# A two-block transformer kernel on one core: the first mixer's convolution, its tap engines and its place between the mLSTM's heads

## The chip, the cores and the metric

The kernel runs on one core of one Trainium2 chip. The time is device microseconds of that core from launch to end, the median of three runs. TensorE is called PE here, VectorE DVE, ScalarE ACT, GpSimd POOL and SyncE SP.

## What is computed

Two stacked blocks of two layers each on 512 tokens of width 1024, with a context of 256 tokens in the first block. The change lies in the first layer's mixer of the first block, which works on all 768 tokens. The part of the reference that matters:

```
a, g, q, k, v, o, gates = split(h @ w_in)
u = dwconv(a * sigmoid(g), conv_w (31 taps, 512 channels), conv_b)
u = silu(layer_norm(u, ln_g, ln_b))
h_seq = mLSTM(q, k, v, gates), forward and backward, 4 heads
        h = num / max(|den|, exp(-m_row))        per head and direction
hm = rms(h_seq) * head_gain * sigmoid(o)
y = concat(u, hm) @ w_out
```

Everything is float32 in and out. A product with weights is three matmuls on PE: each operand is split into a high and a low part of the type fp32r, and high by high, high by low and low by high are added in PSUM. ACT makes the high part of a weight chunk (`whi`, line 287), DVE the low part (`wlo`, line 288).

## The kernel before, in words

Channels (or tokens, inside the mLSTM) lie on the 128 partitions. `mixer0` (line 684) builds the first mixer. One *product* (`fmk_g`, line 385, which calls `fm_g`, line 369) takes one 512 KB chunk of weights, 1024 columns wide, and makes 128 output channels for all 768 tokens: 24 matmuls of 512 columns and 24 of 256.

The 512 channels of the convolution are four blocks of 128. `conv_g` (line 786) makes one block: two products (gate `g` and value `a`; those of block 0 are made earlier, by `first`), a tanh on ACT (line 797), the gated value `up` on DVE (line 801), and then 31 taps over 783 columns (both token segments with padding). With `NPOOL = 10` the taps stand on three engines: DVE does 21 of a block (line 813 the first, line 821 twenty others, each `acc = up[shifted] * weight + acc`), ACT scales ten shifted copies (lines 815 and 818), POOL adds nine of them up in `acc2` (line 819) and adds that to `acc` at the end (line 824). `convt`, the tile between ACT and POOL, has two buffers. `conv_norm` (line 828) is the layer norm over the four blocks: POOL sums the blocks (lines 833 and 835), PE and DVE make the mean, DVE centres (line 855), ACT squares (line 862), POOL sums the squares (line 864), DVE scales (line 870) and adds `ln_b` (line 874), and then comes the SiLU.

The *output gates* are four more products, `th[0]` to `th[3]`, one for each head, with a tanh on ACT (line 717).

The convolution and the gates are one generator, `work` (line 707). `more(n)` (line 782) advances it n steps, and `mixer0` calls it between the four q and k products (`MORE`, line 962), and `mlstm` in each pass. The written order is blocks 0 to 3, gates 0 and 1, the norm, gates 2 and 3. That order is a priority only: a scheduler places each instruction on its engine by its own estimate of the times, and engines then run in the order that it fixed, with semaphores between them. SP loads the weight chunks; the adaptive-norm products of later layers (line 525, `ps_ad`, one 512 KB chunk for two matmuls of 512 columns that run at float32 rate) are a second side work.

`mlstm` (line 964) goes over 4 heads with 6 *passes* each (one for each 128 tokens): PE makes scores (line 997), ACT the decay factors with exp (lines 1014, 1016), DVE multiplies them (line 1021), PE multiplies by v with a column of ones (line 1034), and DVE normalises the result of the pass: copy of the denominators, absolute value, maximum, reciprocal, scaling of the first direction, second direction added (lines 1037 to 1042). Passes 0 and 1 of a head look at 2 blocks of keys, the other four at 6. `v1` is copied out of PSUM by DVE (line 741). At a head's end its result is transposed on PE (line 1056) and multiplied by its output gate (line 1057). The output projection (`ab_o`, from line 747) takes the four convolution blocks as its first four chunks and the heads as the last four.

PSUM has three banks tagged `ml` for scores and results; a pass of six key blocks takes two.

## Time and profile before

| what | us |
|---|---|
| median of three runs | 3781.64 (3776.6 to 3785.46) |
| profiled execution, its own time | 3775.19 |
| its span, first to last instruction | 3773.4 |
| PE busy in the span | 3643.6 |
| first scores of the mLSTM (line 997) | at 246.84 |
| last passes of the mLSTM end, last head transposed | about 424 |

All times in rows are microseconds from the span's start. "Busy" is the time in which an engine has an instruction in work; matmuls overlap, so a matmul's own duration is longer than the step to the next. PEclk is the share of 2.4 GHz that PE was granted; it is 1.0 or 0.5, and values between are means over a stretch. A wait's releaser is inferred from semaphore events.

### The profile page before, as it was taken

To read this page: it belongs to the slowest core of one execution; us is meant where nothing else is said; L and a number is where in the kernel's file an instruction comes from. 1 tells how busy PE (TensorE), PEld (TensorE's weight loads), DVE (VectorE), ACT (ScalarE), POOL (GpSimd) and SP (SyncE) were. 2 spreads that over 40 slices of the span, in tenths; PEclk is the share of its full clock that TensorE was granted. 3 is DMA by queue.
4 is the path that set the end of the run, shared out by engine and by line. 5 is a ranking of instruction groups with operands and counts; after the bars stand their busy time and mean duration, and the time that the engine had idled before them with its cause. 6 is when DMAs were issued, how large, how long until landed. Compare 5 with 4: busy or idle time off the path is not lost. (4 is left out here: it accounts for less than half of the span.)

```text
span 3773.4 us, 50278 instructions
## 1 busy us (share of the span) xinstructions
PE 3643.6 (97%) x19848; PEld 2979.0 (79%) x19848; DVE 2191.9 (58%) x3583; ACT 1430.5 (38%) x2507; POOL 543.4 (14%) x528
## 2 busy tenths in 40 slices
PE   7889999999999999999999999999999999999998
PEld 5667877888877667888877888888887888888887
DVE  6986454444456666655576565555566656545545
ACT  4335332222235555433354333432234433333222
POOL 3540100000025221000221110300022111020001
PEclk9989999999999999999999999999999999999999
DMA  5223323332211010333333322233324333222232
GB/s 194 72 78 115 104 90 117 118 123 63 67 49 44 22 34 23 103 103 96 97 111 101 96 86 77 78 100 101 95 73 130 96 98 93 73 90 90 95 96 78
DMA packets 107388, 336.88 MB, mean 89 GB/s; under 512 B 14864, under 2 KB 19600, under 8 KB 106896
## 3 DMA queue, kind: packets, MB, share of 16 engines
q1 hardware_dynamic: 94864, 316.88, 26.2%
q10 hardware_dynamic: 12288, 16.79, 1.8%
q8 instruction: 156, 2.56, 0.3%
q14 instruction: 80, 0.66, 0.1%
HBM read 310.54 MB, written 2.10 MB: 83 GB/s over the span
## 5 line engine op out<-in xcount | busy, mean ns | idle before, releaser
L287 ACT CAST whi<-raw 128x1024 fp32r<-128x1024 f32 (+2 forms) x488 | 501.7, 1030 | 1148.6 <-PE ps_mm L367 698.6
L288 DVE TENSOR_TENSOR wlo<-raw,whi 128x1024 fp32r<-128x1024 f32 (+2 forms) x488 | 621.6, 1276 | 370.4 <-ACT whi L287 367.6
L367 PE MATMUL ps_mm<-h,whi 128*128 128x512 f32 (+2 forms) x2593 | 642.3, 354 | 20.1 <-ACT cth L797 10.6
L367 PE MATMUL ps_mm<-xg,whi 128*128 128x512 f32 (+1 forms) x1929 | 571.9, 378 | 9.1 <-DVE xg L302 7.0
L367 PEld LDWEIGHTS ps_mm<-h,whi 128*128 128x128 f32 (+1 forms) x2593 | 428.1, 189 | 108.5 <-issue 17.8
L367 PE MATMUL ps_mm<-hid,whi 128*128 128x512 f32 (+1 forms) x1805 | 469.5, 357 | 0.0
L367 PEld LDWEIGHTS ps_mm<-xg,whi 128*128 128x128 f32 x1929 | 357.1, 189 | 80.0 <-DVE xg L302 11.4
L367 PE MATMUL ps_mm<-h,wlo 128*128 128x512 f32 (+2 forms) x1298 | 393.9, 353 | 0.5 <-DVE wlo L288 0.5
L366 PE MATMUL ps_mm<-xg,whi 128*128 128x512 f32 (+1 forms) x1207 | 373.9, 388 | 2.7 <-DVE xg L302 2.7
L367 PE MATMUL ps_mm<-xg,wlo 128*128 128x512 f32 (+1 forms) x966 | 362.0, 377 | 0.5 <-DVE wlo L288 0.5
L367 PEld LDWEIGHTS ps_mm<-hid,whi 128*128 128x128 f32 x1805 | 310.3, 188 | 59.3 <-issue 6.7
L367 PE MATMUL ps_mm<-hid,wlo 128*128 128x512 f32 (+1 forms) x903 | 298.9, 356 | 0.0
L366 PEld LDWEIGHTS ps_mm<-xg,whi 128*128 128x128 f32 x1207 | 219.9, 189 | 49.3 <-issue 5.3
L367 PEld LDWEIGHTS ps_mm<-h,wlo 128*128 128x128 f32 (+1 forms) x1298 | 217.4, 189 | 36.2 <-DVE wlo L288 1.0
L366 PE MATMUL ps_mm<-xg,wlo 128*128 128x512 f32 (+1 forms) x602 | 228.4, 382 | 0.0
L367 PEld LDWEIGHTS ps_mm<-xg,wlo 128*128 128x128 f32 x966 | 182.9, 190 | 33.8 <-DVE wlo L288 1.0
L367 PEld LDWEIGHTS ps_mm<-hid,wlo 128*128 128x128 f32 x903 | 160.4, 189 | 24.9
L1532 POOL TENSOR_TENSOR rsw<-rsw,rope 128x512 f32<-128x512 f32 x64 | 107.7, 1683 | 428.5 <-DMA rsw<-rsw 286.5
L1156 DVE SCALAR_TENSOR_TENSOR xl<-ps_mm,mod,xl 128x512 f32<-128x512 f32 (+1 forms) x102 | 73.0, 717 | 110.7 <-PE ps_mm L367 110.2
L366 PE MATMUL ps_mm<-whi,xg 128*128 128x512 f32 x384 | 132.0, 414 | 0.0
L366 PEld LDWEIGHTS ps_mm<-xg,wlo 128*128 128x128 f32 x602 | 113.8, 189 | 22.2 <-issue 0.7
L821 DVE SCALAR_TENSOR_TENSOR acc<-up,cw,acc 128x783 f32<-128x783 f32 x80 | 124.4, 1555 | 2.2
(572 smaller groups left out, 5833.4 us busy)
## 6 DMA issues: line engine op xcount, KB each, us to landing
raw<-in_fup SPq DMA_DIRECT2D x88, 512.0 KB, 3.5
raw<-in_sup SPq DMA_DIRECT2D x88, 512.0 KB, 3.5
raw<-in_ada SPq DMA_DIRECT2D x80, 512.0 KB, 3.6
raw<-in_l_qk SPq DMA_DIRECT2D x48, 512.0 KB, 3.5
raw<-in_fdn SPq DMA_DIRECT2D x32, 512.0 KB, 3.5
raw<-in_d_v SPq DMA_DIRECT2D x32, 512.0 KB, 3.6
raw<-in_d_gt SPq DMA_DIRECT2D x32, 512.0 KB, 3.5
raw<-in_sdn SPq DMA_DIRECT2D x32, 512.0 KB, 3.5
```

The source lines that it names most:

```text
L287: self.nc.scalar.copy(h[:, :n], r[:, :n])
L288: (lo or self.nc.vector).tensor_tensor(l[:, :n], r[:, :n], h[:, :n].bitcast(F32), ALU.subtract)
L366: return self.nc.tensor.matmul(out, w, x, **k)
L367: return self.nc.tensor.matmul(out, w, x, **k)
L821: nc.vector.scalar_tensor_tensor(acc, u, s, acc, ALU.mult, ALU.add)
L1156: self.pin(nc.vector.scalar_tensor_tensor(xs, o[:, : b - a], self.m(layer, 5, d, int(a < TC)), xs, ALU.mult, ALU.add))
L1532: nc.gpsimd.tensor_tensor(sw, sw, self.SR, ALU.mult)
```

## The change

All 31 taps of a block go to DVE; ACT's scaled copies and POOL's sums of them are gone, with the tiles `conv2` and `convt` for taps. The sums of `conv_norm` (blocks, squares) move from POOL to DVE. The written order of the side work becomes blocks 0 to 2, gates 0 and 1, block 3, the norm, gates 2 and 3, with other step counts (`MORE`). Four pieces move from DVE to ACT: the copies of v, the absolute value of the denominators (one instruction for two), the scaling of the first direction, and the addition of `ln_b`.

```
@@ -705,18 +705,25 @@
             accs, th, mixc = [], [], []
 
             def work():
-                for j in range(4):
-                    accs.append((yield from self.conv_g(mp, j, hs, cw, None if j else made)))
-                yield
-                for j in range(4):
-                    if j == self.NORM:
-                        yield from self.conv_norm(mp, accs, mixc)
+                def gate(j):
                     t = pair()
                     o = yield from self.fmk_g(I["ab_fm"][12 + j], hs, SEG, every=2)
                     for q, u in zip(o, t):
                         nc.scalar.activation(u, q[:, : u.shape[1]], AF.Tanh, scale=0.5)
                     th.append(t)
                     yield
+
+                def conv(j):
+                    accs.append((yield from self.conv_g(mp, j, hs, cw, None if j else made)))
+
+                for j in range(3):
+                    yield from conv(j)
+                yield from gate(0)
+                yield from gate(1)
+                yield from conv(3)
+                yield from self.conv_norm(mp, accs, mixc)
+                yield from gate(2)
+                yield from gate(3)
 
             self.more_work = work()
             self.more(4)
@@ -738,7 +745,7 @@
             for tb, o in enumerate(os):
                 t = mp.tile([P, 4, 129], F32, name=f"v1_{tb}")
                 nc.vector.memset(t[:, :, 128:129], 1.0)
-                nc.vector.tensor_copy(t[:, :, :128], o.rearrange("p (h v) -> p h v", h=4))
+                nc.scalar.copy(t[:, :, :128], o.rearrange("p (h v) -> p h v", h=4))
                 v1.append(t)
             self.side(8)
             self.mlstm(tp, qk[:2], qk[2:], v1, gate, th)
@@ -803,25 +810,15 @@
             )
         yield
         acc = self.tl(mp, [P, L], "acc", bufs=4)
-        acc2 = self.tl(mp, [P, L], "conv2", bufs=2)
-        n = self.NPOOL
-        order = [0, 1] + [w for i in range(CONVW) for w in (2 + i, n + 1 + i) if (w == 2 + i < n + 1) or (w == n + 1 + i < CONVW)]
-        for c, w in enumerate(order):
+        for w in range(CONVW):
             s = cw[:, CONVW * j + w : CONVW * j + w + 1]
             u = up[:, w : w + L]
             if w == 0:
                 nc.vector.tensor_scalar(acc, u, s, self.par("conv_b", j, j + 1), ALU.mult, ALU.add)
-            elif w == 1:
-                nc.scalar.activation(acc2, u, AF.Copy, scale=s)
-            elif w <= n:
-                tt = self.tl(mp, [P, L], "convt", bufs=2)
-                nc.scalar.activation(tt, u, AF.Copy, scale=s)
-                nc.gpsimd.tensor_tensor(acc2, acc2, tt, ALU.add)
             else:
                 nc.vector.scalar_tensor_tensor(acc, u, s, acc, ALU.mult, ALU.add)
-            if c % 4 == 3:
+            if w % 3 == 2:
                 yield
-        nc.gpsimd.tensor_tensor(acc, acc, acc2, ALU.add)
         yield
         return acc
@@ -830,9 +827,9 @@
         nc = self.nc
         L = TA + 15
         s = self.tl(mp, [P, TA + 45], "up", bufs=2)[:, :L]
-        nc.gpsimd.tensor_tensor(s, accs[0], accs[1], ALU.add)
+        nc.vector.tensor_tensor(s, accs[0], accs[1], ALU.add)
         for j in (2, 3):
-            nc.gpsimd.tensor_tensor(s, s, accs[j], ALU.add)
+            nc.vector.tensor_tensor(s, s, accs[j], ALU.add)
         yield
         offs = [0, 128] + [TC + 15 + 128 * i for i in range(4)]
         parts = ((TC, TA, TC + 15), (0, TC, 0))
@@ -861,7 +858,7 @@
             for a, b, o in parts:
                 nc.scalar.activation(t[:, o : o + b - a], accs[j][:, o : o + b - a], AF.Square)
                 if j:
-                    nc.gpsimd.tensor_tensor(q[:, o : o + b - a], q[:, o : o + b - a], t[:, o : o + b - a], ALU.add)
+                    nc.vector.tensor_tensor(q[:, o : o + b - a], q[:, o : o + b - a], t[:, o : o + b - a], ALU.add)
             yield
         R = both(self.rstd([q[:, o : o + P] for o in offs], 512, EPS, "c6"))
         for j in range(4):
@@ -871,7 +868,7 @@
         yield
         for j in range(4):
             y = accs[j]
-            nc.vector.tensor_scalar_add(y, y, self.par("ln_b", j, j + 1))
+            nc.scalar.activation(y, y, AF.Identity, bias=self.par("ln_b", j, j + 1))
             t = self.tl(mp, [P, TA], "cth", bufs=1)
             for a, b, o in parts:
                 v = y[:, o : o + b - a]
@@ -958,8 +955,7 @@
         return gcol, Gcol, FLO
 
     SIDES = (1, 1)
-    NORM = 2
-    MORE = (10, 15, 15, 15)
+    MORE = (14, 14, 14, 14)
 
     def mlstm(self, tp, q, k_, v1, gate, th):
         nc = self.nc
@@ -1026,7 +1022,6 @@
                     end()
                 if ib == 3 and h < 3:
                     nxt = spread(h + 1)
-                den = self.small([P, 2], "lden")
                 rd = self.small([P, 2], "lrd")
                 pn = A[:, :258].rearrange("p (d c) -> p d c", d=2)
                 for d, (s, js) in enumerate(S):
@@ -1034,11 +1029,10 @@
                         nc.tensor.matmul(
                             pn[:, d], s[:, j * P : j * P + P], v1[j][:, h, :], start=(j == js[0]), stop=(j == js[-1])
                         )
-                nc.vector.tensor_copy(den, pn[:, :, 128])
-                nc.vector.scalar_tensor_tensor(rd, den, -1.0, den, ALU.mult, ALU.max)
+                nc.scalar.activation(rd, pn[:, :, 128], AF.Abs)
                 nc.vector.tensor_tensor(rd, rd, FLO[:, ib, :, h], ALU.max)
                 nc.vector.reciprocal(rd, rd)
-                nc.vector.tensor_scalar_mul(hs[:, ib, :], pn[:, 0, :128], rd[:, 0:1])
+                nc.scalar.activation(hs[:, ib, :], pn[:, 0, :128], AF.Copy, scale=rd[:, 0:1])
                 nc.vector.scalar_tensor_tensor(hs[:, ib, :], pn[:, 1, :128], rd[:, 1:2], hs[:, ib, :], ALU.mult, ALU.add)
                 sq = self.tl(tp, [P, P], "hsq")
                 nc.scalar.activation(sq, hs[:, ib, :], AF.Square, accum_out=ss[:, ib : ib + 1])
@@ -1998,7 +1992,6 @@
 
     def run(self, out, stop=None):
         nc, tc, I = self.nc, self.tc, self.I
-        self.NPOOL = 10
```

Rows of the change below carry its own line numbers, some five lower (1034 becomes 1029, 1021 becomes 1017, 821 becomes 819).

How the scheduler then places it, at three places. First DVE around the start of the mLSTM (`acc` with a number is one convolution block, `S` the decay factors, `wlo` a weight chunk's low part, `dg` a diagonal block). Before:

```order
L741 COPY v_2_1755<-ps_ml_1601 128x4x128
L821 SCALAR_TENSOR_TENSOR acc_1523<-up_1334,cw,acc_1523 128x783
L741 COPY v_3_1758<-ps_ml_1602 128x4x128
L741 COPY v_4_1761<-ps_ml_1603 128x4x128
L741 COPY v_5_1764<-ps_st_1604 128x4x128
L821 SCALAR_TENSOR_TENSOR acc_1523<-up_1334,cw,acc_1523 128x783
L1021 TENSOR_TENSOR S_276_1834<-S_276_1834,ps_ml_1831 128x128
L1007 SCALAR_TENSOR_TENSOR dg_1840<-GB_1826,g_TB,con_593 128x128
L1007 SCALAR_TENSOR_TENSOR dg_1889<-GB_1815,g_T_705,con_593 128x128
L1021 TENSOR_TENSOR S_278_1839<-S_278_1839,ps_ml_1831 128x256
```

and of the change:

```order
L819 SCALAR_TENSOR_TENSOR acc_1242<-up_1121,cw,acc_1242 128x783
L288 TENSOR_TENSOR wlo_1502<-raw_1499,whi_1501 128x1024
L1003 SCALAR_TENSOR_TENSOR dg_1849<-GB_1727,g_T_696,con_593 128x128
L819 SCALAR_TENSOR_TENSOR acc_1242<-up_1121,cw,acc_1242 128x783
L1003 SCALAR_TENSOR_TENSOR dg_1856<-GB_1738,g_TB,con_593 128x128
L830 TENSOR_TENSOR up_2451<-acc_611,acc_1021 128x783
L832 TENSOR_TENSOR up_2451<-up_2451,acc_1242 128x783
L288 TENSOR_TENSOR wlo_1508<-raw_1505,whi_1507 128x1024
L1017 TENSOR_TENSOR S_244_1746<-S_244_1746,ps_ml_1743 128x128
L1017 TENSOR_TENSOR S_246_1751<-S_246_1751,ps_ml_1743 128x256
```

Before, the last taps of the fourth block (`acc_1523`) and the copies of v stand ahead of the mLSTM's first multiplication. In the change the third block (`acc_1242`) is the last one ahead of it, with the diagonal blocks already made, two sums for the norm, and no copy of v.

Second DVE in the first head, at its fourth and fifth pass. Before:

```order
L1021 TENSOR_TENSOR S_338_2127<-S_338_2127,ps_ml_2109 128x256
L1007 SCALAR_TENSOR_TENSOR dg_2250<-GB_2087,g_TB,con_593 128x128
L1021 TENSOR_TENSOR S_336_2117<-S_336_2117,ps_ml_2110 128x128
L1021 TENSOR_TENSOR S_338_2127<-S_338_2127,ps_ml_2110 128x256
L1042 SCALAR_TENSOR_TENSOR hs_1829<-ps_ml_2003,lrd_2091,hs_1829 128x128
L1007 SCALAR_TENSOR_TENSOR dg_2316<-GB_2076,g_T_705,con_593 128x128
L1037 COPY lden_2152<-ps_ml_2109 128x2
```

and of the change:

```order
L817 TENSOR_SCALAR acc_2094<-up_1462,cw,par 128x783
L1003 SCALAR_TENSOR_TENSOR dg_2171<-GB_1970,g_T_696,con_593 128x128
L819 SCALAR_TENSOR_TENSOR acc_2094<-up_1462,cw,acc_2094 128x783
L1033 TENSOR_TENSOR lrd_2046<-lrd_2046,g_FLO 128x2
L1003 SCALAR_TENSOR_TENSOR dg_2177<-GB_1981,g_TB,con_593 128x128
L1017 TENSOR_TENSOR S_300_2071<-S_300_2071,ps_ml_2063 128x512
L1017 TENSOR_TENSOR S_302_2082<-S_302_2082,ps_ml_2063 128x256
L819 SCALAR_TENSOR_TENSOR acc_2094<-up_1462,cw,acc_2094 128x783
L1034 RECIPROCAL lrd_2046<-lrd_2046 128x2
L1017 TENSOR_TENSOR S_300_2071<-S_300_2071,ps_ml_2064 128x256
```

The fourth block (`acc_2094`) now starts here: its 31 taps stand one or a few at a time between the instructions of the first two heads, the last of them at the end of the second head. Lines 1037, 1038 and 1041 are gone from DVE.

Third PE in the third head: the end of a pass and the start of the next. Before:

```order
L1034 MATMUL ps_ml_2941<-v_5_1764,S_520_2959 128x129
L997 MATMUL ps_ml_3004<-xl_915,xc_1372 128x128 x2
L997 MATMUL ps_ml_3004<-xl_915,xl_1371 128x128 x2
L997 MATMUL ps_ml_3005<-xl_915,xl_1371 128x128 x2
L525 MATMUL ps_ad_2968<-raw_3285,sc 32x512 x2
L525 MATMUL ps_ad_2968<-raw_3335,sc 32x512 x2
L1034 MATMUL ps_ml_3004<-v_0_1749,S_529_3012 128x129
L1034 MATMUL ps_ml_3004<-v_1_1752,S_529_3012 128x129
```

and of the change:

```order
L1029 MATMUL ps_ml_2539<-v_3_1670,S_404_2554 128x129
L993 MATMUL ps_ml_2540<-xl_915,xl_1261 128x128 x2
L993 MATMUL ps_ml_2591<-xl_915,xc_1262 128x128 x2
L993 MATMUL ps_ml_2591<-xl_915,xl_1261 128x128 x2
L1050 MATMUL ps_st_2460<-con,hs_2118 128x128 x4
L1050 MATMUL ps_st_2466<-con,hs_2118 128x128 x2
L1029 MATMUL ps_ml_2539<-v_4_1673,S_404_2554 128x129
L1029 MATMUL ps_ml_2539<-v_5_1676,S_404_2554 128x129
L993 MATMUL ps_ml_2592<-xl_915,xl_1261 128x128 x2
L1029 MATMUL ps_ml_2591<-v_0_1661,S_412_2599 128x129
```

Before, side matmuls (line 525, `ps_ad`) stand between scores and the products with v. In the change the last product of the side work (gate 3) and a last chunk of line 525 stand at the third head's first scores, and behind them no matmul of either kind until the output projection's first chunk comes up in the fourth head's passes; scores of the pass's second bank (`ps_ml_2540`) stand behind the first products with v.

## Rows read from the trace of the kernel before

**Rows 1.** The page, part 1: busy time of the engines over the whole execution.
```profile
PE 3643.6 (97%) x19848; PEld 2979.0 (79%) x19848; DVE 2191.9 (58%) x3583; ACT 1430.5 (38%) x2507; POOL 543.4 (14%) x528
```

**Rows 2.** Busy time by stretch (span's us; length, engines, PEclk, DMA share, GB/s).
```profile
66.00:246.80 180.80, 143.21 (x783) 114.97 (x781) 172.81 (x128) 65.60 (x103) 103.35 (x47) 0.93 0.21 69
246.80:318.00 71.20, 70.84 (x410) 50.95 (x411) 36.77 (x114) 30.59 (x100) 11.65 (x10) 0.89 0.42 140
318.00:372.00 54.00, 54.00 (x380) 45.24 (x379) 41.50 (x120) 32.21 (x96) 2.64 (x2) 1.00 0.29 96
372.00:424.00 52.00, 49.07 (x331) 40.19 (x330) 31.58 (x105) 22.50 (x76) 2.64 (x2) 1.00 0.38 130
```

**Rows 3.** Waits of PE, 66 to 250 us: total us, times, longest.
```profile
PE ps_mm L367 <- ACT cth L797: 10.6, 2, 7.0
PE ps_mm L367 <- DVE wlo L288: 8.4, 1, 8.4
PE ps_ml L997 <- DVE v L741: 6.7, 2, 6.3
```

**Rows 4.** PE busy in the five half-clock stretches: the last two, and all five.
```profile
244.70:255.00 10.30, 7.84 (x30) 0.50 0.01 2
268.60:275.40 6.80, 6.80 (x30) 0.50 0.26 80
sum 40.90, PE 28.04; mean PE 5.61
```

**Rows 5.** Taps on DVE: ns min/median/max, and the page's group (mean ns).
```profile
L821 DVE SCALAR_TENSOR_TENSOR acc<-up,cw,acc x80: 1021/1035/2734, 72.9 to 249.4; 128x783 f32<-128x783 f32 x80
...
L821 DVE SCALAR_TENSOR_TENSOR acc<-up,cw,acc 128x783 f32<-128x783 f32 x80 | 124.4, 1555 | 2.2
```

**Rows 6.** Instructions in order of time: start, us, engine, line; 107 to 140 us.
```profile
107.04 4.24 DVE L821 SCALAR_TENSOR_TENSOR acc<-up,cw,acc 128x783 f32<-128x783 f32 x4
...
139.98 11.26 DVE L821 SCALAR_TENSOR_TENSOR acc<-up,cw,acc 128x783 f32<-128x783 f32 x5
```

**Rows 7.** Groups, 60 to 250 us: count, busy us, mean ns, idle before.
```profile
L819 POOL TENSOR_TENSOR conv<-conv,convt 128x783 f32<-128x783 f32 x36 | 90.5, 2513 | 25.0 <-ACT convt L818 22.5
...
L818 ACT ACTIVATE convt<-up,cw 128x783 f32<-128x783 f32 x36 | 33.7, 947 | 38.1 <-POOL conv L819 38.0
```

**Rows 8.** Order of time, PE inside one product (three matmuls a chunk).
```profile
147.42 0.39 PE L367 MATMUL ps_mm<-h,wlo 128*128 128x512 f32 x1
...
148.10 0.39 PE L367 MATMUL ps_mm<-h,wlo 128*128 128x512 f32 x1
```

**Rows 9.** A group of PE, 247 to 424 us.
```profile
L525 PE MATMUL ps_ad<-raw,sc 128*32 128x512 f32 x116 | 26.5, 624 | 1.2 <-DMA raw<-in_ada 1.2
```

**Rows 10.** Groups of DVE, 247 to 424 us.
```profile
L1021 DVE TENSOR_TENSOR S<-S,ps_ml 128x256 f32<-128x256 f32 x36 | 14.7, 414 | 4.0 <-PE ps_ml L997 2.7 <-ACT S L1014 1.1
L1021 DVE TENSOR_TENSOR S<-S,ps_ml 128x512 f32<-128x512 f32 x16 | 10.9, 684 | 3.7 <-PE ps_ml L997 3.5
...
L1041 DVE TENSOR_SCALAR hs<-ps_ml,lrd 128x128 f32<-128x128 f32 x24 | 8.3, 347 | 0.5
```

**Rows 11.** A group of ACT, 247 to 424 us.
```profile
L1014 ACT ACTIVATE S<-dg 128x128 f32<-128x128 f32 x47 | 13.9, 297 | 10.4 <-PE ps_ml L1034 8.8 <-DVE dg L1007 1.2 <-DVE lrd L1040 0.2
```

**Rows 12.** Order of time: one pass of the third head, to the next pass.
```profile
371.27 2.17 PE L1034 MATMUL ps_ml<-v,S 128*128 128x129 f32 x18
...
373.38 0.71 PE L997 MATMUL ps_ml<-xl,xc 64*128 64x128 f32 x4
...
373.49 0.16 DVE L1037 COPY lden<-ps_ml 128x2 f32<-128x2 f32 x1 [3.95 <-PE ps_ml L1034]
...
373.93 1.05 PE L997 MATMUL ps_ml<-xl,xl 64*128 64x128 f32 x8
...
376.56 0.34 DVE L1042 SCALAR_TENSOR_TENSOR hs<-ps_ml,lrd,hs 128x128 f32<-128x128 f32 x1
...
377.30 0.94 PE L1034 MATMUL ps_ml<-v,S 128*128 128x129 f32 x6
```

More of the change, by code (lines that the diff above doesn't have):

```diff
@@ L707, in work, with gate @@
             def work():
-                for j in range(4):
-                    accs.append((yield from self.conv_g(mp, j, hs, cw, None if j else made)))
-                yield
-                for j in range(4):
-                    if j == self.NORM:
-                        yield from self.conv_norm(mp, accs, mixc)
+                def gate(j):
                     t = pair()
@@ L719, in work, with conv @@
                     yield
+                def conv(j):
+                    accs.append((yield from self.conv_g(mp, j, hs, cw, None if j else made)))
+                for j in range(3):
+                    yield from conv(j)
+                yield from gate(0)
+                yield from gate(1)
+                yield from conv(3)
+                yield from self.conv_norm(mp, accs, mixc)
+                yield from gate(2)
+                yield from gate(3)
             self.more_work = work()
@@ L740, in mixer0 @@
                 nc.vector.memset(t[:, :, 128:129], 1.0)
-                nc.vector.tensor_copy(t[:, :, :128], o.rearrange("p (h v) -> p h v", h=4))
+                nc.scalar.copy(t[:, :, :128], o.rearrange("p (h v) -> p h v", h=4))
                 v1.append(t)
@@ L805, in conv_g @@
         acc = self.tl(mp, [P, L], "acc", bufs=4)
-        acc2 = self.tl(mp, [P, L], "conv2", bufs=2)
-        n = self.NPOOL
-        order = [0, 1] + [w for i in range(CONVW) for w in (2 + i, n + 1 + i) if (w == 2 + i < n + 1) or (w == n + 1 + i < CONVW)]
-        for c, w in enumerate(order):
+        for w in range(CONVW):
             s = cw[:, CONVW * j + w : CONVW * j + w + 1]
@@ L813, in conv_g @@
                 nc.vector.tensor_scalar(acc, u, s, self.par("conv_b", j, j + 1), ALU.mult, ALU.add)
-            elif w == 1:
-                nc.scalar.activation(acc2, u, AF.Copy, scale=s)
-            elif w <= n:
-                tt = self.tl(mp, [P, L], "convt", bufs=2)
-                nc.scalar.activation(tt, u, AF.Copy, scale=s)
-                nc.gpsimd.tensor_tensor(acc2, acc2, tt, ALU.add)
             else:
                 nc.vector.scalar_tensor_tensor(acc, u, s, acc, ALU.mult, ALU.add)
-            if c % 4 == 3:
+            if w % 3 == 2:
                 yield
-        nc.gpsimd.tensor_tensor(acc, acc, acc2, ALU.add)
         yield
@@ L832, in conv_norm @@
         s = self.tl(mp, [P, TA + 45], "up", bufs=2)[:, :L]
-        nc.gpsimd.tensor_tensor(s, accs[0], accs[1], ALU.add)
+        nc.vector.tensor_tensor(s, accs[0], accs[1], ALU.add)
         for j in (2, 3):
-            nc.gpsimd.tensor_tensor(s, s, accs[j], ALU.add)
+            nc.vector.tensor_tensor(s, s, accs[j], ALU.add)
         yield
@@ L863, in conv_norm @@
                 if j:
-                    nc.gpsimd.tensor_tensor(q[:, o : o + b - a], q[:, o : o + b - a], t[:, o : o + b - a], ALU.add)
+                    nc.vector.tensor_tensor(q[:, o : o + b - a], q[:, o : o + b - a], t[:, o : o + b - a], ALU.add)
             yield
@@ L873, in conv_norm @@
             y = accs[j]
-            nc.vector.tensor_scalar_add(y, y, self.par("ln_b", j, j + 1))
+            nc.scalar.activation(y, y, AF.Identity, bias=self.par("ln_b", j, j + 1))
             t = self.tl(mp, [P, TA], "cth", bufs=1)
@@ L960 @@
     SIDES = (1, 1)
-    NORM = 2
-    MORE = (10, 15, 15, 15)
+    MORE = (14, 14, 14, 14)
     def mlstm(self, tp, q, k_, v1, gate, th):
@@ L1028, in mlstm @@
                     nxt = spread(h + 1)
-                den = self.small([P, 2], "lden")
                 rd = self.small([P, 2], "lrd")
@@ L1036, in mlstm @@
                         )
-                nc.vector.tensor_copy(den, pn[:, :, 128])
-                nc.vector.scalar_tensor_tensor(rd, den, -1.0, den, ALU.mult, ALU.max)
+                nc.scalar.activation(rd, pn[:, :, 128], AF.Abs)
                 nc.vector.tensor_tensor(rd, rd, FLO[:, ib, :, h], ALU.max)
                 nc.vector.reciprocal(rd, rd)
-                nc.vector.tensor_scalar_mul(hs[:, ib, :], pn[:, 0, :128], rd[:, 0:1])
+                nc.scalar.activation(hs[:, ib, :], pn[:, 0, :128], AF.Copy, scale=rd[:, 0:1])
                 nc.vector.scalar_tensor_tensor(hs[:, ib, :], pn[:, 1, :128], rd[:, 1:2], hs[:, ib, :], ALU.mult, ALU.add)
@@ L2000, in run @@
         nc, tc, I = self.nc, self.tc, self.I
-        self.NPOOL = 10
         self.stop = stop
```

## The prediction

> **What bounds the kernel now.** I read the page first: PE is busy 97% of the span [rows 1], so the whole kernel gains only where PE idles or runs slowly, or where its work shrinks. The change takes no matmul away. What can be won is therefore PE's idle time and slow clock in the mixer, and nothing else.
>
> The stretches come next [rows 2]. From 66 to 246.8 us, where the convolution runs ahead of the mLSTM, PE is busy 143.2 of 180.8: 37.6 idle. DVE is busy 172.8 of it, so DVE is the bound there. From 246.8 to 424, through the four heads, PE idles 0.4 + 0.0 + 2.9 = 3.3: there PE is the bound, at a DVE share of 62% (109.9 of 177.2). The waits name the ends of the idle time [rows 3]: 10.6 for a tanh on ACT, 8.4 for a low part on DVE, 6.7 for a copy of v on DVE. Then the clock: in five stretches PE was granted 1.2 instead of 2.4 GHz, each behind idle time or matmuls of few columns, and was busy 28.0 us in them [rows 4]. At twice the clock this would take half, so they cost about 14.0, of which 7.3 lie past 244 us. Together 37.6 + 3.3 + 14.0 = **54.9 us** stand to be won at most.
>
> Why DVE is full: a tap takes 1.02 to 1.04 us by minimum and median, but 1.555 in the mean [rows 5]. Four taps with POOL silent take 4.24, or 1.06 each; five taps during POOL's sums take 11.26, or 2.25 each [rows 6]. The 36 sums on POOL keep it busy 90.5 us, and ACT waits 38.0 us for POOL to free `convt` [rows 7]; the tanh that PE waits for stands behind those copies on ACT's queue.
>
> **The taps.** Ahead of the mLSTM stand three blocks instead of four, 90 taps of the main kind instead of 80. With POOL silent they cost 90 x 1.06 = 95.4 instead of 80 x 1.555 = 124.4. DVE's work there becomes 172.8 - 124.4 + 95.4 = 143.8 us, with two sums of blocks for the norm (2.1) in place of the copies of v; less where POOL held other instructions too. That is no longer above PE's own work.
>
> **PE's work ahead of the mLSTM.** The order holds 11 products there instead of 10 (gates 0 and 1 and one product of block 3, for two of block 3). In a product three 512-column matmuls take 0.68 us from start to start [rows 8], 0.227 each, and half of that with 256 columns: 24 x 0.227 + 24 x 0.113 = 8.2 us. Six more chunks of line 525 stand there, 12 instructions of 0.23 (26.5 us for 116) [rows 9]: 2.7. At full clock PE needs 143.2 - 6.7 + 8.2 + 2.7 = 147.4. PE (147) and DVE (144) then nearly balance. Idle time left: 0 if queues never meet, 12 (a third of today's) if they often do; I take **5**, since ACT's queue is freed of 40 scaled copies. The mLSTM would start near 66 + 147 + 5 = 218 instead of 246.8. PE's later work shrinks by the same 10.9.
>
> **First and second head.** All remaining side matmuls stand here: three products (25 us) and most of line 525. DVE takes on the fourth block, 31 x 1.06 = 33 us, and loses 12 times lines 1037, 1038 and 1041 (0.16 + 0.16 + 0.35) [rows 10, 12] = 8. With its 62% share today it has the room, and the taps stand singly between the mLSTM's instructions, so one of them delays a multiplication by about 1 us while PE has side work. I keep today's 3.3, rounded to **4**; a bound is 12, if each of the 12 passes lost one tap's time.
>
> **Third and fourth head.** Here PE has no side work, and DVE and ACT get the whole norm. Floors, from today's rows:
> PE: a pass over six blocks needs 2.17 + about 1.6 = 3.8 [rows 12], a pass over two a third, 1.3; 8 x 3.8 + 4 x 1.3 = 36, with broadcasts, transposes and the first projection chunks some 51.
> DVE: 16 passes end between 318 and 424, with 41.5 + 31.6 = 73.1 of DVE [rows 2]; 12 passes take 55, less 8 for the three lines gone, plus 13 for the norm (centring, squares' sums and scaling, 11 tile halves of 0.684 and 11 of 0.414 [rows 10], and a sum of 1.06): 60.
> ACT: 12/16 of 54.7 is 41 [rows 2], plus 12 scalings like an exp of the same size (0.297) [rows 11], 12 absolute values (not in this trace; no dearer than that, no less than 0.1), the squares and `ln_b`: 55.
> So DVE sets the floor, 60. The ceiling: a six-block pass takes 6.03 today (371.27 to 377.30) [rows 12], when normalising waits 3.4 us through DVE's queue (373.49 to 376.90); 8 x 6.03 + 4 x 3 = 60, plus the norm's 13 and waits of the two moved steps between ACT and DVE, 12 x 1 = 12: 85. I take **73**, midway, as the three floors are near each other and every pass goes from PE to ACT to DVE and back twice. PE is then idle 73 - 51 - 4 (projection chunks that fit in) = **18**, between 5 and 30.
>
> **Clock.** With such idle time PE may be granted half its clock at times; I take **3** us lost, as in one stretch of 6.8 us [rows 4]. The row nearest speaks for little: from 372 to 424, with 2.9 idle, the clock is 1.00 [rows 2], though side matmuls fill the passes there. The Trainium skill's page "TensorE: Matmul & The Clock Gate", section "A second HAM failure mode: psum-queue depth-cycling", tells of a kernel that goes round PSUM banks, idles briefly between groups and has its clock swing between both levels. No run here shows that; by it the loss would not be 3 but that of the clock rival below.
>
> **Moves with one answer.** Copies of v on ACT (six, on an engine busy 65.6 of 180.8 [rows 2] with 40 copies fewer) cost nothing unless ACT is late at the mLSTM's start: 6 x 0.6 = 3.6 at most. POOL's queue only empties. SP's loads swap places; the DMA share is 0.21 to 0.42 [rows 2], and I cost them at nothing.
>
> **The sum.** Won 54.9, left 5 + 4 + 18 + 3 = 30: 25 us. The profiled execution took 3775.2 us, 6.4 under the median of the runs shown (3781.6); 25 less on the median is **3757 us** (3750 on the profiled one). With the bounds of the heads alone the gain is 13 to 38, or 3744 to 3769.
>
> **Rivals.**
> *Heads keep up* (15%): the third and fourth head run at DVE's floor, 5 idle, and 2 ahead of the mLSTM. Left 14, gain 41: 3741. For it: normalising no longer queues three times on DVE. Against: three floors within 9 us of each other.
> *Heads give it back* (9%): without side work passes go at today's mean pace, 106 us for 16, so 80 for 12, plus the norm's 13: 93, idle 38, with 8 for the clock. Left 55, gain 0: 3782. Against: today's pace is set by PE being full.
> *The clock falls* (6%): PE idles in each pass of the last two heads and is granted 1.2 GHz for all of them. Its 51 us become about 95, with 13 of waits 108 instead of 73: 35 more, 10 slower than before: 3792. From about 70% of that stretch at half clock it decides the sign. For it: 6.8 us at half clock at 268.6 came without an idle gap, behind matmuls of few columns, and the norm's means and broadcasts, of that kind, stand here. Against: the 1.00 at 372 to 424.
> *Taps stay slow* (4%): POOL was not what held them. 90 x 1.555 keeps DVE at 188 ahead of the mLSTM, PE idles as today, and the heads' losses come on top: 3805. Against: every tap with POOL silent is near 1.03 [rows 5, 6].
>
> **How the numbers follow.** Forecast 66%. A measurement of this kernel tells about 0.2% (7.6 us) from no change. Faster by more: 66 + 15 and a little of the second rival, 0.83; within: 0.08; slower: 0.09. The range goes from near the first rival to short of the second: 3738 to 3776.
>
> **What would show it.** Taps at 1.03 to 1.06 with no group near 2.5; the first scores near 218 us; PE without idle of several us ahead of them; no half clock there; in the last two heads PE idle 5 to 30 with DVE busy over 80%. The prediction is wrong if the scores start after 235, if PE idles over 30 in the heads, or if half clock spreads over them.

## The result, and the profile after

The changed kernel takes 3749.8 us (median of 4 runs, 3746.2 to 3751.9) against 3781.5 (3776.6 to 3785.5): ratio 0.9924, 95% interval 0.9911 to 0.9936. (The quotient of the two medians, 0.9916, lies in that interval.) A second series gave 0.9925 (0.9913 to 0.9936). The profiled executions, 3775.2 before and 3751.9 after, differ by 23.3 us.

Page of the changed kernel, part 1, to lay beside [rows 1]; PE's work is the same:

```profile
PE 3645.8 (97%) x19848; PEld 2979.1 (79%) x19848; DVE 2150.1 (57%) x3550; ACT 1409.4 (38%) x2525; POOL 429.8 (11%) x479
```

Busy time by stretch, changed kernel: ahead of the scores, then each of the four heads, of which each ends where its result is transposed on PE (columns as in [rows 2]):

```profile
66.00:218.90 152.90, 149.19 (x860) 120.55 (x859) 120.92 (x141) 38.50 (x81) 0.39 (x6) 1.00 0.26 86
218.90:275.80 56.90, 53.49 (x344) 36.29 (x343) 34.09 (x87) 26.62 (x103) 2.05 (x1) 1.00 0.61 203
275.80:325.00 49.20, 46.39 (x299) 37.12 (x298) 40.73 (x80) 25.24 (x81) 1.59 (x2) 0.97 0.49 163
325.00:356.80 31.80, 27.57 (x208) 25.45 (x208) 25.72 (x74) 23.28 (x73) 2.64 (x2) 0.96 0.06 18
356.80:389.40 32.60, 31.12 (x182) 27.23 (x181) 19.37 (x49) 16.77 (x55) 1.32 (x1) 0.88 0.11 33
```

The first scores start at 218.9 us instead of 246.8. PE is busy 149.2 of 152.9 ahead of them, DVE only 120.9, POOL 0.4.

Taps of the changed kernel, ns minimum, median and maximum (against [rows 5]):

```profile
L819 DVE SCALAR_TENSOR_TENSOR acc<-up,cw,acc x120: 936/1029/1037, 73.2 to 314.1; 128x783 f32<-128x783 f32 x120
```

Waits of PE in the changed kernel, 66 to 389.4 us (total, times, longest), in place of [rows 3]:

```profile
PE ps_ad L525 <- DMA raw<-in_ada: 3.0, 4, 1.2
PE ps_ml L993 <- DVE hs L1036: 2.9, 2, 1.5
PE ps_ml L1029 <- DVE lrd L1034: 2.2, 1, 2.2
PE ps_ml L1029 <- DVE S L1017: 2.0, 2, 1.2
```

No tap is held up any more, and none of the three long waits is left. The first update of the residual stream from the mixer's output (the start of its line in `made`) comes at 393.1 us instead of 426.8. So the mixer gives 33.7 us, 10 more than the profiled executions differ: something later takes them back.

### The profile page after: what moved, and what is told of

It reads as the page before. It is cut to its first block, busy times and chain, and to the rows that moved or that the text cites. A ratio compares the mean times of both kernels' runs of the same rounds, so it can differ in the third digit from the quotient of the medians.

```text
span 3749.9 us, 50176 instructions
## 1 busy us (share of the span) xinstructions
PE 3645.8 (97%) x19848; PEld 2979.1 (79%) x19848; DVE 2150.1 (57%) x3550; ACT 1409.4 (38%) x2525; POOL 429.8 (11%) x479
## 5 line engine op out<-in xcount | busy, mean ns | idle before, releaser
L288 DVE TENSOR_TENSOR wlo<-raw,whi 128x1024 fp32r<-128x1024 f32 (+2 forms) x488 | 613.0, 1258 | 389.6 <-ACT whi L287 387.0
L367 PE MATMUL ps_mm<-xg,wlo 128*128 128x512 f32 (+1 forms) x966 | 362.5, 378 | 0.5 <-DVE wlo L288 0.5
```

What stands on the lines that cost most here:

```text
L288: (lo or self.nc.vector).tensor_tensor(l[:, :n], r[:, :n], h[:, :n].bitcast(F32), ALU.subtract)
L367: return self.nc.tensor.matmul(out, w, x, **k)
```

## The experiments

A start differs by some 4 us between executions, so two marks are counted from the moment at which DVE has made the first half (512 columns) of the first block's gated value `up` (67.2 us before, 67.5 after): the first scores, and the first residual update. "Half clock" is the sum of the stretches at 1.2 GHz from 66 us to that update; in them a matmul of 512 columns starts every 427 ns instead of every 227 (medians of the kernel before), so that about half of the time that PE is busy there is lost, and half is what is counted below. "h stretch" is first start to last end of the 1128 matmuls that read `h` between 1447 and 1819 us.

| kernel | us | ratio (95%) | scores | update | half clock | h stretch |
|---|---|---|---|---|---|---|
| before | 3781.5 | 1 | 179.6 | 359.6 | 41.0 | 320.6 |
| after | 3749.8 | 0.9924 (.9911-.9936) | 151.4 | 325.6 | 13.7 | 328.5 |
| e1_taps_only | 3738.9 | 0.9895 (.9882-.9909) | 136.4 | 320.8 | 3.4 | 321.0 |
| e2_move_only | 3791.6 | 1.0037 (1.0025-1.0049) | 185.7 | 362.5 | 47.8 | 328.3 |
| e3_small_back | 3744.4 | 0.9916 (.9902-.9931) | 151.4 | 324.3 | 6.8 | 322.2 |
| e4_pool_beside | 3764.7 | 0.9965 (.9953-.9977) | 165.6 | 347.3 | 44.4 | 327.1 |
| e5_pool_idle_sums | 3780.4 | 1.0010 (1.0001-1.0020) | 177.6 | 365.1 | 44.4 | 320.7 |
| e5_sums_on_dve | 3740.4 | 0.9905 (.9890-.9920) | 137.1 | 316.9 | 3.4 | 320.9 |
| e6_taps_and_norm | 3742.7 | 0.9908 (.9894-.9922) | 136.4 | 325.5 | 10.2 | 322.2 |
| e7_pass_steps_back | 3744.4 | 0.9907 (.9893-.9922) | 151.5 | 324.1 | 6.8 | 320.9 |
| e8_after_again | 3747.4 | 0.9925 (.9913-.9936) | 151.4 | 324.4 | 10.2 | 327.4 |
| e8_v_back | 3753.3 | 0.9932 (.9920-.9944) | 151.4 | 330.9 | 27.3 | 328.5 |
| e8_norm_on_pool | 3752.9 | 0.9937 (.9924-.9950) | 151.4 | 339.1 | 34.1 | 321.4 |
| e9_address_kept | 3742.7 | 0.9908 (.9892-.9923) | 151.4 | 326.2 | 13.7 | 322.1 |

### Which part of the change gives the time

**e1_taps_only.** The kernel before, with the loop of `conv_g` as in the change (`yield` still after every fourth tap).

```diff
-        for c, w in enumerate(order):
+        for w in range(CONVW):
...
-        nc.gpsimd.tensor_tensor(acc, acc, acc2, ALU.add)
```

> The kernel before, with one part of the change: all taps on VectorE. The blocks stay in their old places (all four ahead of the mLSTM), the four small moves and the norm's sums stay undone. Theory (the gain comes from the moved block; the taps alone swap one load for another): ahead of the mLSTM VectorE would do 120 taps of 1.03 us = 124 us in place of 80 of 1.555 us = 124 us, so its share of the stretch does not shrink and the first scores stay within 8 us of 246.8 us; time 3774 to 3788 us. Rival (ScalarE's queue, blocked by GpSimd, was what held PE): the tanh no longer stands behind scaled copies, PE gets back the 10.6 us that it waited for it, first scores near 236, time 3768 to 3773 us.

Both were wrong: the taps alone give the whole gain and more. The stretch ahead of the scores:

```profile
66.00:200.60 134.60, 132.90 (x760) 108.21 (x758) 126.17 (x148) 26.82 (x57) 0.40 (x6) 1.00 0.25 80
```

DVE is as full as before (126 of 134.6, or 94%), and yet PE idles only 1.7 us. A full DVE thus does not bound PE: most of what fills it are taps that nobody waits for yet, and 22 of 124 run beside the heads.

**e2_move_only.** The changed kernel, its taps on three engines as in the kernel before (one `yield` after every third).

```diff
-        for w in range(CONVW):
...
+        for c, w in enumerate(order):
...
+                nc.scalar.activation(tt, u, AF.Copy, scale=s)
+                nc.gpsimd.tensor_tensor(acc2, acc2, tt, ALU.add)
```

> The changed kernel with its taps put back on three engines (ten of each block as a ScalarE copy and a GpSimd sum); the moved block, the gates, the small moves and the norm's sums on VectorE stay changed. Theory (moving the block is what counts): ahead of the mLSTM VectorE has 60 taps at 1.555 us = 93 us in place of 90 at 1.03 = 93 us, so the stretch costs it the same; first scores at 219 to 226 us, and time 3748 to 3760 us. Rival (the taps count on their own): ScalarE's queue stays blocked by GpSimd, its products' tanh come late, first scores at 230 to 240, time 3762 to 3775 us. In both, taps beside GpSimd's sums are near 2.5 us again.

Both were too low. The move without the taps is slower than the kernel before: taps up to 2.68 us again, scores at 185.7, PE 26 us idle ahead of them, though one block fewer stands there. Of the 14 us that it is slower, the mixer gives 2.9 (362.5 instead of 359.6 at the update) and the h stretch 7.7, for a reason that is found further down; the rest was not followed.

**e3_small_back.** The changed kernel with `nc.scalar` turned back to `nc.vector` in the copies of v, `ln_b`, the absolute value (two instructions again, with the tile `lden`) and the scaling (the latter two as in the diff of e7_pass_steps_back).

```diff
-                nc.scalar.copy(t[:, :, :128], o.rearrange("p (h v) -> p h v", h=4))
+                nc.vector.tensor_copy(t[:, :, :128], o.rearrange("p (h v) -> p h v", h=4))
...
-            nc.scalar.activation(y, y, AF.Identity, bias=self.par("ln_b", j, j + 1))
+            nc.vector.tensor_scalar_add(y, y, self.par("ln_b", j, j + 1))
```

> The changed kernel with the four small moves undone: copies of v, absolute value of the denominators, scaling of the first direction and ln_b on VectorE again. Theory (VectorE's queue is the last wait of the passes in the third and fourth head): twelve passes there get back 0.67 us of VectorE each = 8 us and four ln_b of about 0.9 us, and six copies of v delay the first scores by 2 to 4 us: time 3756 to 3766 us, third and fourth head 66 to 72 us instead of 64.4. Rival (each moved step adds a trip between ScalarE and VectorE that costs what it saves): 3746 to 3753 us.

The time (3744.4) lies below both ranges, on the rival's side, and the mixer is the same to 1.3 us: in it the small moves give nothing and cost nothing.

### What held PE: a full queue, ScalarE, or GpSimd

**e4_pool_beside.** Idle work on GpSimd in the changed kernel:

```diff
+            if j < 2 and w % 3 == 0:
+                d = self.tl(mp, [P, L], "convt", bufs=2)
+                if j == 0:
+                    nc.gpsimd.tensor_tensor(d, u, u, ALU.add)
+                else:
+                    nc.gpsimd.tensor_copy(d[:, :1], u[:, :1])
+                    nc.gpsimd.memset(d[:, 1:], 0.0)
```

> The changed kernel with work on GpSimd that nobody waits for: beside the taps of the first block eleven sums of 783 columns that read SBUF, beside those of the second eleven fills of 782 columns that read nothing, beside those of the third none. Theory (a GpSimd instruction that reads SBUF holds up VectorE's taps, which read two tiles there): taps beside the sums take near 2.5 us, about one in two, so the first block's taps cost 14 to 17 us more, those beside the fills stay at 1.03; first scores 6 to 14 us later than 218.9, time 3756 to 3764 us. Rival 1 (any GpSimd instruction holds them): the second block's taps are long as well. Rival 2 (the long taps before came from waits on ScalarE's copies): all taps stay at 1.03 and the time at 3747 to 3753 us. By the Trainium skill's page 'SBUF — State Buffer', on the shared port pair, the sums hold the taps and the fills do not.

DVE in order of time (start, us, instruction), first during GpSimd's eleven sums, the last row during its fills:

```profile
74.25 1.47 DVE L903 COPY g_f<-gt 128x48 f32<-128x48 f32 x1
75.64 2.32 DVE L819 SCALAR_TENSOR_TENSOR acc<-up,cw,acc 128x783 f32<-128x783 f32 x1
...
93.06 1.03 DVE L819 SCALAR_TENSOR_TENSOR acc<-up,cw,acc 128x783 f32<-128x783 f32 x1
```

GpSimd of the same kernel:

```profile
68.05 20.69 POOL L823 TENSOR_TENSOR convt<-up 128x783 f32<-128x783 f32 x11 [7.15 <-DVE up L808]
...
93.00 1.43 POOL L826 MEMSET convt<- 128x782 f32 x2
```

Sums that read SBUF hold the tap (2.32 instead of 1.03) and even a copy of 48 columns (1.47; in the changed kernel 0.19). Fills hold nothing: none of the 23 taps that ran beside them, or beside the one-column copy ahead of each, took over 1.04. That is the theory's mechanism but not its size, for only six taps are long, which costs them some 7 us instead of 14 to 17. The time came just past its upper end, and it is no clean measure: PE is busy 22.5 us longer at half clock than in the changed kernel (36.1 instead of 13.6), and 20.5 of that lie from 330.8 to 351.3 us, long after the sums. The Trainium skill's page "SBUF — State Buffer", section "SBUF: two separate sides", says that DVE and GpSimd share a pair of ports which an instruction holds for its whole length; the trace agrees, for these sums and fills.

**e5_pool_idle_sums** and **e5_sums_on_dve** take the two suspects of the kernel before apart. The first is e1_taps_only with ten idle sums a block on GpSimd; the second the kernel before with the taps' sums on VectorE.

```diff
+            if 0 < w <= 20 and w % 2:
+                d = self.tl(mp, [P, L], "convt", bufs=2)
+                nc.gpsimd.tensor_tensor(d, u, u, ALU.add)
```

> The kernel before with all taps on VectorE (as in the run with the taps alone), and on GpSimd ten sums of 783 columns beside each block's taps, as many as it made before, whose results nobody reads; ScalarE makes no scaled copies. Theory (the hold-up of VectorE's in-order queue by GpSimd's sums is what kept PE waiting): the first scores start at 230 to 248 us instead of 200.6, first residual update of the mixer's output near 410 to 430 us instead of 385.0, time 3762 to 3785 us. Rival (ScalarE's queue, blocked by waits for GpSimd, is what kept PE waiting): taps are long, yet few stand ahead of what PE needs; first scores at 200 to 215, time 3739 to 3752 us.

```diff
-                nc.gpsimd.tensor_tensor(acc2, acc2, tt, ALU.add)
+                nc.vector.tensor_tensor(acc2, acc2, tt, ALU.add)
...
-        nc.gpsimd.tensor_tensor(acc, acc, acc2, ALU.add)
+        nc.vector.tensor_tensor(acc, acc, acc2, ALU.add)
```

> The kernel before, with GpSimd's sums of the taps moved to VectorE: ScalarE still makes ten scaled copies of each block and waits for VectorE to free their two buffers, and no GpSimd instruction stands beside the taps. Theory (GpSimd's hold-up): VectorE does 31 instructions of near 1.03 us per block, as with the taps alone; first scores at 198 to 212 us, first residual update near 385 to 392, time 3738 to 3750 us. Rival (ScalarE's blocked queue): the copies wait for VectorE as they did for GpSimd, the products' tanh and the splits of weights stand behind them, first scores at 225 to 245 us, time 3760 to 3780 us.

The theory held both times. Ahead of the scores, first with idle sums on GpSimd, then with the needed sums on VectorE (columns as in [rows 2]):

```profile
66.00:241.50 175.50, 140.96 (x757) 112.78 (x756) 171.41 (x145) 27.29 (x58) 83.58 (x46) 0.90 0.20 66
```

```profile
66.00:204.70 138.70, 136.15 (x786) 111.37 (x784) 130.86 (x155) 65.28 (x102) 2.27 (x7) 1.00 0.25 80
```

Sums that nobody reads bring back the time of before (3780.4), though ScalarE makes no copy. Their update is 44.3 us later than in e1_taps_only. Of this 32.8 us are idle time of PE; the rest fits the clock, as PE is busy 22.9 us longer at half clock (26.3 instead of 3.4). PE's waits in that kernel, 66 to 241.5 us, are for a tanh and a low part as in [rows 3], and for the gated value:

```profile
PE ps_mm L367 <- ACT cth L797: 10.9, 2, 10.6
PE ps_mm L367 <- DVE wlo L288: 9.6, 1, 9.6
PE ps_mm L367 <- DVE up L801: 4.9, 1, 4.9
```

How a sum that nobody waits for gets to PE is seen in its order of time on ACT, and then on DVE:

```profile
206.46 1.06 ACT L287 CAST whi<-raw 128x1024 fp32r<-128x1024 f32 x1 [7.93 <-PE ps_mm L367]
```

```profile
208.62 15.34 DVE L812 SCALAR_TENSOR_TENSOR acc<-up,cw,acc 128x783 f32<-128x783 f32 x7
223.88 2.51 DVE L288 TENSOR_TENSOR wlo<-raw,whi 128x1024 fp32r<-128x1024 f32 x1
```

The high part of a weight is ready at 207.5. Its low part stands behind seven taps in DVE's queue; at 1.03 they would take 7.2 us, held up they take 15.3, and the split itself 2.5 instead of 1.2. PE stands idle for 9.6 us from 216.8 on.

The longest wait, 10.6 us for a tanh, comes the same way by a detour over a weight load. Rows of DVE, SP's waits from 60 to 110 us, and ACT in the kernel with idle sums:

```profile
90.44 1.22 DVE L288 TENSOR_TENSOR wlo<-raw,whi 128x1024 fp32r<-128x1024 f32 x1
```

```profile
SPq L279 <- DVE wlo L288: 26.3, 4, 19.1
```

```profile
95.37 1.04 ACT L287 CAST whi<-raw 128x1024 fp32r<-128x1024 f32 x1 [14.45 <-DMA raw<-in_ab_fm]
96.32 0.87 ACT L797 ACTIVATE cth<-ps_mm 128x512 f32<-128x512 f32 x2
```

The high part of a chunk is ready at 80.0, but its low part starts only at 90.44, behind taps and small instructions that the sums hold. Only then is the chunk's buffer free, for which SP has waited 19.1 us; the next chunk lands late, ACT's cast waits 14.45 us for it, and the tanh stands behind that cast. In e1_taps_only the low part starts as its high part is ready (79.53), SP's longest such wait is 8.2 us, and PE waits 0.3 us for that tanh.

In the second kernel ScalarE still makes its copies and waits for their buffers, now for VectorE:

```profile
ACT convt L818 <- DVE conv L819: 19.4, 15, 3.0
```

PE idles 2.6 us ahead of its scores. So ScalarE's copies cost nothing; GpSimd's sums cost it all, by holding up VectorE's queue.

**e6_taps_and_norm.** e1_taps_only with `conv_norm`'s sums on VectorE, as in the change.

```diff
-            nc.gpsimd.tensor_tensor(s, s, accs[j], ALU.add)
+            nc.vector.tensor_tensor(s, s, accs[j], ALU.add)
...
```

> The run with the taps alone, and the convolution norm's sums on VectorE too, so that GpSimd does nothing of the convolution but fill the pads. Theory: the sums on GpSimd (some 12 us of its time between 257 and 300 us) hold VectorE there while PE has side work and idles little, so both ways cost the same: 3735 to 3743 us, first residual update within 3 us of 385.0. Rival (the hold-up reaches PE there too): first residual update 4 to 8 us earlier, time 3729 to 3735 us.

The theory's time came (3742.7), but neither mark: the update is 4.7 us later, with 2.8 more idle and 6.8 more at half clock, and the intervals of the times overlap. Taking the hold-up of these sums away gained nothing, so where they stand in e1_taps_only it does not reach PE.

### Where the changed kernel loses 8 us

e3_small_back was 5 us faster with the same mixer, so the loss had to lie later.

**e7_pass_steps_back.** Of the small moves, only those in the passes are undone.

```diff
+                den = self.small([P, 2], "lden")
...
-                nc.scalar.activation(rd, pn[:, :, 128], AF.Abs)
+                nc.vector.tensor_copy(den, pn[:, :, 128])
+                nc.vector.scalar_tensor_tensor(rd, den, -1.0, den, ALU.mult, ALU.max)
...
-                nc.scalar.activation(hs[:, ib, :], pn[:, 0, :128], AF.Copy, scale=rd[:, 0:1])
+                nc.vector.tensor_scalar_mul(hs[:, ib, :], pn[:, 0, :128], rd[:, 0:1])
```

> The changed kernel with two of the four small moves undone, those inside each pass of a head: absolute value of the denominators and scaling of the first direction on VectorE again; copies of v and ln_b stay on ScalarE. Theory (the 5 us that the small moves cost come from the two added trips between PE's results, ScalarE and VectorE in each pass): first residual update at 387 to 389 us instead of 393.1, time 3742 to 3747 us. Rival (the copies of v on ScalarE, late at the mLSTM's start, and ln_b cost it): first residual update at 392 to 394, time 3747 to 3752 us.

The time is the theory's, but its reason is not: counted from the mark, the update is within 1.5 us of the changed kernel's (324.1 and 325.6).

**e8_after_again** is unchanged, and **e8_v_back** undoes one small move:

```diff
-                nc.scalar.copy(t[:, :, :128], o.rearrange("p (h v) -> p h v", h=4))
+                nc.vector.tensor_copy(t[:, :, :128], o.rearrange("p (h v) -> p h v", h=4))
```

> The changed kernel once more, on the same chip as the two next to it. In its first profile the matmuls of 512 columns between 1450 and 1810 us started every 237 ns in most of that stretch, in the profiles of the run with the taps alone and of the kernel before every 227 ns, at a granted clock of 1.00 in all; that is some 8 us. Theory A (this comes and goes between executions): runs spread from 3739 to 3752 us, median 3743 to 3750. Theory B (it belongs to this kernel): again 3746 to 3752 us, and 237 ns in the profile. First residual update of the mixer's output at 393 in both.

> The changed kernel with one of the small moves undone: the six copies of v on VectorE again. Undoing all four brought the first scores from 218.9 to 215.1 us and the first residual update from 393.1 to 388.0, undoing the two in the passes only to 218.8 and 391.4. Theory (the copies of v on ScalarE are most of what the small moves cost): first scores at 214 to 216, first residual update at 388 to 391, time 2 to 5 us below the changed kernel beside it. Rival (ln_b, or only the two steps in the passes): first scores at 218 to 220, first residual update at 392 to 394, time within 2 us of the changed kernel.

Theory B held: the spacing came again, and the h stretch is 327.4. (The steps are 229 and 237 ns in nearly equal number, 233.3 in the mean.) The scores of both stand at 151.4 after the mark, so the 3.8 us that the second run was built on were only a later start of one execution, and its scores at 215.8 in absolute time prove nothing. At the update the second is 5.3 us later than the first profile of the changed kernel, with 13.6 us more at half clock. That is neither theory's, and the copies of v are no cost that these runs show.

**e8_norm_on_pool.** e3_small_back with the norm's sums back on GpSimd (the diff of e6_taps_and_norm turned round).

> The changed kernel with the four small moves undone and the norm's sums back on GpSimd: what is left of the change is the taps on VectorE and the moved block and gates. Theory (with the taps on VectorE the order of the blocks and gates decides nothing): first residual update within 4 us of the 385.0 of the run with the taps alone, time 3736 to 3744 us. Rival 1 (the moved block is worth something once GpSimd is out of the way): first residual update at 376 to 381, time 3729 to 3735. Rival 2 (the norm's sums on GpSimd now stand in the third and fourth head and hold VectorE where it sets the pace): first residual update at 391 to 397, time 3745 to 3752.

The update came at 402.6, past every range, with 34.1 us at half clock. The time came just past rival 2's range (3752.9), but most of it through the clock: PE was busy 30.7 us at half clock instead of 6.8 in e3_small_back, which costs some 12 of the 14.8. Why the clock fell there stays open.

**e9_address_kept.** By then the five profiles without the tile `lden` (changed kernel twice, e2, e4, e8_v_back) had an h stretch of 327.1 to 328.5 us, the eight others 320.6 to 322.2. (The text below miscounts the latter as six.) The kernel is the changed one, with one line:

```diff
+                self.small([P, 2], "lden")
                 rd = self.small([P, 2], "lrd")
```

> The changed kernel with one line more: the small tile that held a copy of the denominators is still taken (128 bytes of a partition in all its buffers), though nothing uses it. Without it every tile that is taken later lies 128 bytes lower, but the h tiles of the stretch from 1450 to 1810 us do not; the order of PE's instructions is the same. Theory (a matmul of 512 columns starts every 233 ns in the mean instead of 227 where its two operands differ by 128 in their addresses modulo 256): in all five kernels without this tile the 237 ns spacing stood there, in the six with it never; with the tile back, 227 ns, 6 to 9 us shorter from first to last matmul there, and time 3737 to 3744 us with the marks of the mixer unchanged (first residual update 388 to 393). Rival (the two steps on ScalarE cause it in another way, or it comes by chance): 237 ns stays, time 3746 to 3752 us.

Matmuls that read `h` there, first in the changed kernel, then with the tile kept (ns minimum, median, maximum, first and last start):

```profile
L367 PE MATMUL ps_mm<-h,whi x707: 278/392/561, 1452.8 to 1780.7; 128*128 128x512 f32 x164, 128*128 128x256 f32 x13
```

```profile
L367 PE MATMUL ps_mm<-h,whi x697: 283/389/497, 1467.4 to 1774.9; 128*128 128x512 f32 x164, 128*128 128x256 f32 x11
```

The theory held: the h stretch is 322.1, the profiled run 3743.0 instead of 3751.9, the mixer the same. The median (3742.7) is better too, though the intervals overlap.

The best version found is e1_taps_only: 3738.9 us, its interval just below that of the changed kernel. e5_sums_on_dve (3740.4) cannot be told from it.

## Why the prediction was right, and where its steps were not

- **Taps.** Right: they take 1.03 us, and none is near 2.5. The 90 of the main kind ahead of the scores keep DVE busy 89.7 us, where 95.4 were priced. *Taps stay slow* is out.
- **Ahead of the mLSTM.** Right in size: PE busy 149.2 (147.4 predicted), idle 3.7 (5), scores at 218.9 (218). One term is right by luck: three more chunks of line 525 stand there (48 rows of the profile against 36), not six, but a chunk shows as four rows, not two. DVE's 143.8 was far too high, at 120.9, for the sums had held more than taps: the small instructions of 48 columns for the mLSTM's gates took 11.9 us in all before and take 2.2 now, and a weight's split took 1.65 us and takes 1.22. The splits ahead of the scores, before and after:

```profile
L288 DVE TENSOR_TENSOR wlo<-raw,whi 128x1024 fp32r<-128x1024 f32 x14 | 23.0, 1648 | 0.9 <-ACT whi L287 0.9
```

```profile
L288 DVE TENSOR_TENSOR wlo<-raw,whi 128x1024 fp32r<-128x1024 f32 x15 | 18.2, 1221 | 8.8 <-ACT whi L287 8.7
```

- **"DVE is the bound there"** failed as a reason. In e1_taps_only DVE is 94% busy and PE runs. What counted was how long the instructions ahead of a split or a product stand in the queue. So the credit for a block less ahead was wrong. With the taps on three engines the rest of the change loses 2.9 us at the update (e2_move_only). With them on VectorE, the new order alone gives 1.2 us where the norm's sums are on VectorE (325.5 in e6_taps_and_norm, 324.3 in e3_small_back), and loses 18.3, most of it by the clock, where they are on GpSimd (320.8 in e1_taps_only, 339.1 in e8_norm_on_pool).
- **"The tanh stands behind those copies on ACT's queue"** failed: without copies PE waits 10.9 us for it (e5_pool_idle_sums), with them 1.8 (e5_sums_on_dve). It stood behind a weight's cast whose load came late.
- **First and second head.** 4 us of idle time were predicted, 6.2 came.
- **Third and fourth head.** 18 us of idle time were predicted, 5.7 came; the stretch took 64.4 us instead of 73, with DVE busy 45.1 of it (70%, not over 80). The mis-sized step is DVE's floor of 60, for two reasons. It counted twelve passes, but only ten are normalised between the second head's transposes and the fourth's (the third head's two short passes come earlier), so that 64.4 stands for somewhat less work than 73 was meant for. And it took DVE's mean pace from 318 to 424 us and added the norm's 13, but that stretch of the kernel before held the norm's scaling (line 870) and `ln_b` already, and five weight splits. ACT's floor of 55 was too high too, at 40.1; its absolute values, which no row of before shows, take 0.17 us each. Three views show the two reasons. The first is the stretch between the same transposes in the kernel before, 63.7 us with DVE busy 40.4. The second is a line of the passes in the changed kernel, there ten times. The third is groups of DVE from 318 to 424 us in the kernel before (busy us, mean ns).

```profile
359.40:423.10 63.70, 60.85 (x418) 51.19 (x417) 40.41 (x130) 31.04 (x100) 2.64 (x2) 1.00 0.31 106
```

```profile
L1033 DVE TENSOR_TENSOR lrd<-lrd,g_FLO 128x2 f32<-128x2 f32 x10 | 1.6, 155 | 2.8 <-ACT lrd L1032 2.8
```

```profile
L288 DVE TENSOR_TENSOR wlo<-raw,whi 128x1024 fp32r<-128x1024 f32 x5 | 6.0, 1219 | 0.0
...
L870 DVE SCALAR_TENSOR_TENSOR acc<-acc,par,ps_st 128x512 f32<-128x512 f32 (+1 forms) x8 | 4.3, 607 | 0.9 <-PE ps_st L443 0.9
...
L874 DVE TENSOR_SCALAR acc<-acc,par 128x783 f32<-128x783 f32 x4 | 2.4, 621 | 0.0
```

- **Clock.** A loss of 3 us was predicted; 13.7 us at half clock cost 6.8, all in and just ahead of the last two heads. The swing over the whole stretch, of the clock rival and of the rule weighed there, did not come.
- **The sum.** Left over are 3.7 + 6.2 + 5.7 + 6.8 = 22.4 of 54.9, which makes 32.5; the update shows 33.7. That is midway between the forecast's 25 and the 41 of *heads keep up*; in the last two heads it is that rival's idle time (5). The h stretch then takes back 7.9, which no step foresaw. So the mixer was forecast some 8 us too slow and the h stretch was left out. These two errors cancel, and the time was right partly by luck.

## What to carry to other kernels

Ask of a busy engine not how full it is but what stands in its queue ahead of the instruction that another engine waits for, and how long each of those takes there. Work given to GpSimd was not free here when it read SBUF beside VectorE: sums that nobody reads cost as much as those that are needed. Try the parts of a change singly, since here one gave it all, and after removing even a tiny tile compare stretches that the edit did not touch.

## What the runs showed of the hardware that was not expected

- Without 128 bytes of small tiles, the weight tiles lie 128 bytes lower in each partition, and the `h` tiles of the h stretch stay. In the compiled programs an `h` tile is at 196576 in both; a weight tile is at 47968 in the changed kernel and 48096 with the tile. Modulo 256 that is 224 for `h` against 96 and 224, and the other `h` and weight tiles of the stretch have the same remainders. With unequal remainders the 512-column matmuls started every 233.3 ns in the mean, with equal ones every 226.7, at a granted clock of 1.00 in both. In the changed kernel those that read `hid` (remainder 96, as its weights) started every 226.9, so the weights' remainder alone is not the cause. Whether 256 is the right modulus was not tried, and unequal remainders are not the only cause of long steps: matmuls with `xg` as weights took 232 ns in the mean with equal remainders, in both.
- GpSimd's sums held not only taps but a VectorE copy of 48 columns from 0.19 to 1.47 us.
- Time at half clock in the mixer went from 6.8 us (e3_small_back) to 34.1 (e8_norm_on_pool) when only the norm's sums moved from VectorE to GpSimd. It decided the difference between some of these kernels, and its cause was not found.
